# One more slot in a shared buffer pool, and a filter spectrum loaded in three parts

## The chip, the cores and the metric

The kernel runs on one core of a Trainium2 chip. The core has a matrix engine (TensorE, PE in the rows, with PEld for its weight loads), a vector engine (VectorE, DVE), an engine for casts, copies and function tables (ScalarE, ACT), a general one (GpSimd, POOL), and SyncE (SP), which issues nearly all DMA transfers in the order of its program. Each engine works through its own list of instructions in order, and waits at an instruction until the semaphores that it names have come. The metric is the device time of the program in microseconds, as the median of several executions.

## The reference

Two layers of a diffusion trunk over 640 tokens (512 latent ones and 128 of context) of width 1024. Every layer is: RMS norm and modulation, SwiGLU channel mixer, then a token mixer of three parallel parts, then a second channel mixer. The modulation (nine vectors of 1024 for each layer and each of two conditions) is a product of a condition vector with a matrix, 'adaLN' below. Cut to what matters here:

```
def fft_conv(z, k):                      # z (B, L, C), k (2L, C)
    zf = jnp.fft.rfft(z, n=2 * L, axis=1)
    kf = jnp.fft.rfft(k, n=2 * L, axis=0)
    return jnp.fft.irfft(zf * kf[None], n=2 * L, axis=1)[:, :L]

def hyena_mixer(u, sw, sb, filt, bias_d):
    v, x1, x2 = jnp.split(short_conv(u, sw, sb), 3, axis=-1)
    z = v
    for o, gate in enumerate((x1, x2)):
        z = gate * (fft_conv(z, filt[:, o]) + bias_d[o] * z)

def trunk_layer(x, cond, p, pos, ctx_kv):
    mod = silu(cond) @ p['ada_w'] + p['ada_b']
    x = x + 0.5 * g1 * swiglu(rmsnorm(x) * (1 + sc1) + sh1, ...)
    u = (rmsnorm(x) * (1 + sc2) + sh2) @ p['w_in']       # split into pool | attention | hyena
    x = x + g2 * (concat(pool, attention, hyena_mixer(...)) @ p['w_out'])
    x = x + 0.5 * g3 * swiglu(rmsnorm(x) * (1 + sc3) + sh3, ...)
```

The filter `k` depends on the weights alone. So each layer has two FFT convolutions, one after the other (`o` = 0 and 1), since the second takes the gated output of the first.

## The kernel before

**Layout.** Activations lie with features on the 128 partitions and tokens along the row. All large products are made of three matmuls each (high by high, high by low, low by high part): `split` casts a tile to its high part on ACT (L295) and takes the difference for the low part on DVE (L296). Weight tiles (`raw`, 128x512) are loaded by SP, split, and used by PE; they have pools of their own.

**The slot pool.** Almost every other temporary of the kernel comes from one pool, `sp` (L213, L227, L233): one tag, `SLOTS` = 45 buffers of 2560 bytes per partition. The buffers are handed out in rotation: a new tile takes the buffer of the tile that was allocated 45 allocations before, and its first writer waits until the last instruction that touches that older tile is done. The writer may be a DMA. SP then stands at that DMA, and every later transfer in its program with it.

**The FFT convolution** (`conv_step_old`, L1068). Both transforms are products with tables. The steps of one convolution are: SP loads four tables for the way in (`tab`, `load_full(0, 4)`, L261) and five tiles of the filter's spectrum (`kf`, `filter_tiles`, L957 to L961) that the prologue left in DRAM. PE transposes `z` (`ztp`), and ACT copies it out (`zt`, `ztc`, L1080, L1085). Two frequency halves follow (`fi` = 0 and 1): PE makes `zf` (8 products each), ACT copies the odd part (`zod`, L1100), DVE forms sum and difference (`zp`, `zm`, L1102, L1103), and `cmul` multiplies them by the filter: `zp` by `kf[fi]`, `zm` by `kf[2 + fi]`. One `cmul` is five DVE instructions (L969, L971 twice, L973, L974; tiles `cw`, `cw2`, `cy`). DVE then makes `pp` and `pmn` (L1108, L1109). The context part is multiplied by `kf[4]` (`zcs`). For the way back SP loads four more tables (`load_full(4, 8)`, L261), and PE makes `yt` from `pp`, `pmn` and these tables: the first half of the products with `pp` takes the first and the second table, the other half the third and the fourth.

**The mixer.** The two convolutions, attention and pooling are generators, and a string (`MIXP`) says in which order they are advanced. The output projection (`raw` from `in_wout`) and the first weights of the next channel mixer (`ex`) are loaded beside the second convolution.

**adaLN.** 240 dot products of 1024 elements run on DVE as one instruction each (`tensor_tensor_reduce`, L410), spread over three of the channel mixers. The instruction also writes an elementwise product that nobody reads, `junk`. Before, `junk` has one buffer of its own (128x1024 bf16, 2048 bytes per partition).

**Order.** A scheduler with priorities orders the instructions of each engine when the program is built. It knows the buffers of the pools, so a change in the number of buffers, or in what is allocated from them, moves instructions elsewhere too.

Of the kernel before, what the change touches and what calls it, by code (L numbers as in the profile page):

```python
# [13 lines left out]
BF16 = mybir.dt.bfloat16  # L14
# [3 lines left out]
P = 128  # L18
# [14 lines left out]
PROT = 8  # L33
AG0 = (1, 0, 2)
MIXT = 70
SLOTS = 45
PF = 8
WB = 5
EXB = 7
# [144 lines left out]
def hybrid_kernel(ctx: ExitStack, tc: tile.TileContext, a, depth=2, fc=22):  # L184
# [27 lines left out]
    wp = ctx.enter_context(tc.tile_pool(name="wp", bufs=4))  # L212
    sp = ctx.enter_context(tc.tile_pool(name="sp", bufs=SLOTS))  # L213
    tp = ctx.enter_context(tc.tile_pool(name="tp", bufs=2))
# [8 lines left out]
    def nm(s):  # L223
        count[0] += 1
        return f"{s}{count[0]}"

    def slot(n=NCOL, dt=F32, name="s"):  # L227
        return sp.tile([P, n], dt, tag="s", name=nm(name))
# [4 lines left out]
    def slot3(x, y, dt=F32, name="s"):  # L233
        return sp.tile([P, x, y], dt, tag="s", name=nm(name))

    def tiny(n, name="t", bufs=4):
        return tp.tile([P, n], F32, tag=f"{name}{n}", bufs=bufs, name=nm(name))
# [4 lines left out]
    def mix(n=512, name="mx"):  # L242
        return acc(n, mx, name)
# [13 lines left out]
    def load_full(q0, q1, name="tfi"):  # L257
        ts = []
        for q in range(q0, q1):
            t = slot3(2, 256, name="tab")  # L260
            DMA.dma_start(out=t.rearrange("p a b -> p (a b)"), in_=a[name][q])  # L261
            ts.append(t)
        return ts
# [24 lines left out]
    def PR(l, name):  # L288
        lo, hi = PAR_COLS[name]
        return par[l][:, lo:hi]  # L290
# [83 lines left out]
    def bias(l, g):  # L374
        return PR(l, "adab").rearrange("p (g s c r) -> p g s c r", g=9, s=2, c=4)[:, g]
# [21 lines left out]
    def ada_group(l, g):  # L397

        def load(n):
            raw = wp.tile([P, 1024], F32, tag="araw", bufs=ARAWB, name=nm("araw"))  # L400
            DMA.dma_start(out=raw, in_=a["adat"][l * 9 + g - len(AG0), n])
            ada_raw[l, g, n] = raw

        def step(n):
            raw = ada_raw[l, g, n // 2]
            i, r = n // 2, n % 2
            c, s = i // 2, i % 2
            junk = tp.tile([P, 1024], BF16, tag="junk", bufs=1, name=nm("junk"))
            with tc.issue_after(pace[0]) if pace else nullcontext():
                V.tensor_tensor_reduce(out=junk, in0=raw, in1=condb[:, r], scale=1.0, scalar=bias(l, g)[:, s, c, r:r + 1],  # L410
                                       op0=ALU.mult, op1=ALU.add, accum_out=mods[l][:, g, c, s, r:r + 1])
            if n == 2 * DC - 1:
                done.add((l, g))

        for n in range(2 * DC):
            ada_q.append(((lambda n=n: load(n // 2)) if n % 2 == 0 else None, lambda n=n: step(n)))
# [41 lines left out]
    class Norm:  # L458
# [13 lines left out]
        def stat(self, half):  # L472
            if self.key[::3] in done:
                self.affine()
            s = ssq[half]
            tot = mix(3, "tot")
            for t, o in enumerate((0, P, HT - P)):
                PE.matmul(out=tot[:, t:t + 1], lhsT=s[:, o:o + P], rhs=ones[:, 0:1], start=True, stop=True)
            var = tiny(3, "var")
            V.tensor_scalar(out=var, in0=tot, scalar1=1.0 / 1024.0, scalar2=EPS, op0=ALU.mult, op1=ALU.add)  # L480
            rs = tiny(3, "rs")
            G.tensor_tensor(out=rs, in0=var, in1=mhalf, op=ALU.pow)
            self.rs = rs
# [470 lines left out]
            self.keep(k, 4)  # L954
            yield

    def filter_tiles(l, o):  # L957
        flat = [slot3(2, 256, name="kf") for _ in range(5)]
        for j, t in enumerate(flat):
            DMA.dma_start(out=t.rearrange("p a b -> p (a b)"), in_=store[l, 2 * j + o])  # L960
        return flat  # L961

# [14 lines left out]
    def conv_step(l, o, z, gate, out):  # L977
        rl, rlc = filt[l]
        tf = [load_tables("fwd", 0, 4)]
        kf = filter_tiles(l, o)  # L980
        hb = PR(l, "hb")
        zt = [(slot3(2, 256, F32R, name="zt"), slot3(2, 256, F32R, name="ztl")) for _ in range(2)]
# [85 lines left out]
    def conv_step_old(l, o, z, gate, out):  # L1068
        rl, rlc = filt[l]
        tf = load_full(0, 4)  # L1070
        kf = filter_tiles(l, o)
        hb = PR(l, "hb")
        zt = [slot3(2, 256, name="zt") for _ in range(2)]
        for pa in range(2):
            ps = mix(512, "ztp")
            for i in range(2):
                for c in range(2):
                    t0 = pa + i * 256
                    PE.transpose(out=ps[:, (i * 2 + c) * P:(i * 2 + c + 1) * P], in_=z[c][:, t0:t0 + 255:2], identity=ident)
            S.copy(out=zt[pa].rearrange("p a b -> p (a b)"), in_=ps)  # L1080
        zc = slot(256, name="ztc")
        ps = mix(256, "ztp")
        for c in range(2):
            PE.transpose(out=ps[:, c * P:(c + 1) * P], in_=z[c][:, LAT:T], identity=ident)
        S.copy(out=zc, in_=ps)  # L1085
        yield
        pq = []
        for fi in range(2):
            fs = slice(fi * P, (fi + 1) * P)
            eo = []  # L1090
            for pa in range(2):
                ps = mix(512, "zf")
                for c in range(2):
                    for i in range(2):
                        PE.matmul(out=ps[:, c * 256:(c + 1) * 256], lhsT=tf[pa * 2 + i][:, c, fs], rhs=zt[pa][:, i, :],
                                  start=(i == 0), stop=(i == 1))
                eo.append(ps)
            with tc.high_priority(offset=min(CVP, tc.cur_priority)):
                od = slot(512, name="zod")
                S.copy(out=od, in_=eo[1])  # L1100
                zp, zm = slot(512, name="zp"), slot(512, name="zm")
                V.tensor_tensor(out=zp, in0=od, in1=eo[0], op=ALU.add)  # L1102
                V.scalar_tensor_tensor(out=zm, in0=od, scalar=-1.0, in1=eo[0], op0=ALU.mult, op1=ALU.add)  # L1103
                y = cmul(zp, kf[fi], o, 0)
                yp = cmul(zm, kf[2 + fi], o, 1)
                pp, pm_ = slot3(2, 256, name="pp"), slot3(2, 256, name="pmn")
                for q in range(2):
                    V.tensor_tensor(out=pp[:, q], in0=y[:, q], in1=yp[:, 1 - q], op=ALU.add)  # L1108
                    V.tensor_tensor(out=pm_[:, q], in0=y[:, q], in1=yp[:, 1 - q], op=ALU.subtract)  # L1109
            pq.append((pp, pm_))  # L1110
            if fi == 0:
                yield
        ti, vs = load_full(4, 8), []
        psc = mix(512, "zfc")
        for c in range(2):
            PE.matmul(out=psc[:, c * 256:(c + 1) * 256], lhsT=tcx[:, c, :], rhs=zc, start=True, stop=True)
        zcs = slot(512, name="zcs")
        S.copy(out=zcs, in_=psc)
        yc = cmul(zcs, kf[4], o, 0)
        yield  # L1120
        for c in range(2):
            cs = slice(c * P, (c + 1) * P)
            ps = mix(512, "yt")
            for pa in range(2):
                n = 0
                for fi in range(2):
                    for q in range(2):
                        PE.matmul(out=ps[:, pa * 256:(pa + 1) * 256], lhsT=pq[fi][pa][:, q, cs], rhs=ti[fi * 2 + q][:, pa, :],
                                  start=(n == 0), stop=(n == 3))
                        n += 1  # L1130
            pc = mix(128, "ytc")
            for q in range(2):
                PE.matmul(out=pc, lhsT=yc[:, q, cs], rhs=tcx[:, q, :], start=(q == 0), stop=(q == 1))
            v = slot(T, name="yv")
            S.activation(out=v[:, 0:LAT].rearrange("p (t a) -> p a t", a=2), in_=ps.rearrange("p (a t) -> p a t", a=2),
                         func=AF.Identity, scale=rl[:, o * 2 + c:o * 2 + c + 1])
            S.activation(out=v[:, LAT:T], in_=pc, func=AF.Identity, scale=rlc[:, o * 2 + c:o * 2 + c + 1])
            vs.append(v)
        yield
        gate = gate()  # L1140
        for c in range(2):
            u, v = slot(T, name="yu"), vs[c]
            V.scalar_tensor_tensor(out=u, in0=z[c], scalar=hb[:, o * 2 + c:o * 2 + c + 1], in1=v, op0=ALU.mult, op1=ALU.add)
            w = slot(T, name="yw")
            V.tensor_tensor(out=w, in0=u, in1=gate[c], op=ALU.mult)
            out.append(w)
        yield
# [663 lines left out]
```

## Time and profile before

| what | value |
|---|---|
| median of 3 runs | 2406.22 us (2406.14 to 2408.6) |
| profiled execution, its own time | 2408.28 us |
| its span, first to last instruction | 2406.5 us |
| PE busy | 2363.9 us, 98% |
| DVE busy | 1919.6 us, 80% |
| ACT busy | 1094.1 us, 45% |
| mean traffic | 112 GB/s |
| mean granted clock of TensorE | 0.993 |

The span is what the rows' times count in; the execution's own time is 1.78 us longer than it. PE is busy for nearly all of the span, so the places where it stands still are the ones to look at; each idle piece is listed with the instruction or transfer that ended it.

### The profile page before, as it was taken

What the parts mean: (1) busy time and instruction counts of PE and PEld (TensorE: products, weight loads), DVE (VectorE), ACT (ScalarE), POOL (GpSimd) and SP (SyncE); (2) the same over time, 40 slices, a digit from 0 to 9 for tenths busy, and PEclk for the clock granted to TensorE, in tenths of its full rate; (3) what the DMA queues carried; (4) which work ended last, traced back from release to release, by engine and by line L of the source; (5) the groups of instructions that cost most, each with busy time, mean ns of one, the idle gap of its engine ahead of it and who ended that gap; (6) DMA issues with size and microseconds to landing.
All of it is one profiled execution on the core that took longest, in us unless ns stands there. A gap on an engine that the chain in (4) does not pass through costs nothing.

```text
span 2406.5 us, 41068 instructions
## 1 busy us (share of the span) xinstructions
PE 2363.9 (98%) x15576; PEld 2240.9 (93%) x15576; DVE 1919.6 (80%) x3885; ACT 1094.1 (45%) x2228; POOL 18.2 (1%) x46
## 2 busy tenths in 40 slices
PE   8999999999989999999999999999998999999999
PEld 3799999999877999999999999999987799999999
DVE  7888888996786798888989889898778678567583
ACT  4654352534345553453535435253434555335251
POOL 0000000000000000000000000000000000000000
PEclk9999999999989999999999999999999999999999
DMA  9434434353310235344343343534231022222222
GB/s 320 173 101 128 134 117 155 107 172 114 102 45 14 71 110 162 124 125 144 115 137 108 119 136 115 166 110 158 91 112 54 18 71 80 79 84 78 85 68 90
DMA packets 132646, 270.37 MB, mean 112 GB/s; under 512 B 15002, under 2 KB 24924, under 8 KB 132320
## 3 DMA queue, kind: packets, MB, share of 16 engines
q1 hardware_dynamic: 132448, 267.75, 34.8%
q8 instruction: 122, 2.00, 0.4%
q14 instruction: 76, 0.62, 0.1%
HBM read 259.56 MB, written 8.13 MB: 111 GB/s over the span
## 4 chain that ended last, share of the span: by engine, by line
PE 88%; DVE 6%; issue 2%; DMA 1%; ACT 1%; SPq 1%; POOL 0%; POOLq 0%; DVEq 0%; ACTq 0%
PE mm L205 74%; PE Z L205 5%; PE yt L205 1%; PE o L205 1%; PE pt L209 1%; DVE junk L410 1%; PE fk L205 1%; PE mx L205 1%; PE ada L205 1%; PE zf L205 1%; DVE kwl L296 0%; DMA kf<-store 0%; DVE wlo L296 0%; PE rsb L205 0%; DVE rp L1308 0%
## 5 line engine op out<-in xcount | busy, mean ns | idle before, releaser
L205 PE MATMUL mm<-hhi,whi 128*128 128x320 f32 x1440 | 448.4, 311 | 1.1 <-ACT u L1224 1.1
L295 ACT CAST whi<-raw 128x512 fp32r<-128x512 f32 (+1 forms) x394 | 238.7, 606 | 463.3 <-PE mm L205 423.0
L205 PE MATMUL mm<-hlo,whi 128*128 128x320 f32 x1440 | 446.3, 310 | 0.0
L205 PE MATMUL mm<-hhi,wlo 128*128 128x320 f32 x1440 | 446.0, 310 | 0.0
L205 PE MATMUL mm<-alo,whi 128*128 128x320 f32 x1198 | 370.8, 310 | 0.8 <-DVE alo L296 0.8
L205 PE MATMUL mm<-ahi,whi 128*128 128x320 f32 x1198 | 370.8, 310 | 0.0
L205 PE MATMUL mm<-ahi,wlo 128*128 128x320 f32 x1198 | 370.7, 309 | 0.0
L296 DVE TENSOR_TENSOR wlo<-raw,whi 128x512 fp32r<-128x512 f32 (+1 forms) x394 | 263.3, 671 | 75.7 <-ACT whi L295 71.3
L410 DVE CUSTOM_DVE_ANT_0 junk<-araw,condb,par 128x1024 bf16<-128x1024 f32 x240 | 307.4, 1281 | 2.1 <-DMA araw<-in_adat 0.8
L205 PEld LDWEIGHTS mm<-hhi,whi 128*128 128x128 f32 x1440 | 270.5, 188 | 5.9 <-ACT u L1224 2.8
L205 PEld LDWEIGHTS mm<-hlo,whi 128*128 128x128 f32 x1440 | 270.8, 188 | 1.9 <-issue 1.8
L205 PEld LDWEIGHTS mm<-hhi,wlo 128*128 128x128 f32 x1440 | 270.5, 188 | 1.4 <-issue 1.4
L205 PE MATMUL mm<-tlo,whi 128*128 128x320 f32 x864 | 267.4, 309 | 0.0
L205 PE MATMUL mm<-thi,whi 128*128 128x320 f32 x864 | 267.4, 309 | 0.0
L205 PE MATMUL mm<-thi,wlo 128*128 128x320 f32 x864 | 267.3, 309 | 0.0
L205 PEld LDWEIGHTS mm<-alo,whi 128*128 128x128 f32 x1198 | 225.0, 188 | 1.0 <-DVE alo L296 1.0
L205 PEld LDWEIGHTS mm<-ahi,whi 128*128 128x128 f32 x1198 | 225.0, 188 | 0.1
L205 PEld LDWEIGHTS mm<-ahi,wlo 128*128 128x128 f32 x1198 | 225.0, 188 | 0.0
L295 ACT CAST whi<-ex 128x512 fp32r<-128x512 f32 x216 | 134.2, 621 | 188.0 <-PE mm L205 175.6
L296 DVE TENSOR_TENSOR wlo<-ex,whi 128x512 fp32r<-128x512 f32 x216 | 149.2, 691 | 32.6 <-ACT whi L295 28.4
L295 ACT CAST whi<-ws 128x512 fp32r<-128x512 f32 x144 | 89.4, 621 | 162.2 <-PE mm L205 123.1
L205 PEld LDWEIGHTS mm<-thi,whi 128*128 128x128 f32 x864 | 162.3, 188 | 0.0
(263 smaller groups left out, 4704.2 us busy)
## 6 DMA issues: line engine op xcount, KB each, us to landing
araw<-in_adat SPq DMA_DIRECT2D x120, 512.0 KB, 3.6
raw<-in_wgu SPq DMA_DIRECT2D x208, 256.0 KB, 3.1
ex<-in_wgu SPq DMA_DIRECT2D x144, 256.0 KB, 2.7
raw<-in_wd SPq DMA_DIRECT2D x128, 256.0 KB, 2.7
raw<-in_win SPq DMA_DIRECT2D x56, 256.0 KB, 3.0
ar<-in_ada SPq DMA_DIRECT2D x48, 256.0 KB, 5.4
raw<-in_wd SPq DMA_DIRECT2D x64, 192.0 KB, 2.6
tab<-in_tfi SPq DMA_DIRECT2D x32, 256.0 KB, 3.9
```

The costliest lines, as they stand in the source:

```text
L205: cls.order(nc.tensor.matmul(**k))
L209: cls.order(nc.tensor.transpose(**k))
L295: S.copy(out=hi, in_=src)
L296: V.tensor_tensor(out=lo, in0=src, in1=hi.bitcast(F32), op=ALU.subtract)
L410: V.tensor_tensor_reduce(out=junk, in0=raw, in1=condb[:, r], scale=1.0, scalar=bias(l, g)[:, s, c, r:r + 1], op0=ALU.mult, op1=ALU.add, ac ...
```

## The change

Three things: `SLOTS` goes from 45 to 46; `junk` is allocated from the slot pool (and the buffers of one tiny tile, `var`, go from four to two); and the five loads of the filter's spectrum are made in three parts, tiles 0 and 2 at the start of the convolution, 1 and 3 after the matmuls of the first frequency half, tile 4 after those of the second.

```
-SLOTS = 45
+SLOTS = 46
...
-            junk = tp.tile([P, 1024], BF16, tag="junk", bufs=1, name=nm("junk"))
+            junk = slot(1024, BF16, "junk")
...
-            var = tiny(3, "var")
+            var = tiny(3, "var", 2)
...
-    def filter_tiles(l, o):
-        flat = [slot3(2, 256, name="kf") for _ in range(5)]
-        for j, t in enumerate(flat):
+    def filter_tiles(l, o, which=range(5)):
+        flat = {j: slot3(2, 256, name="kf") for j in which}
+        for j, t in flat.items():
             DMA.dma_start(out=t.rearrange("p a b -> p (a b)"), in_=store[l, 2 * j + o])
...
-        kf = filter_tiles(l, o)
+        kf = filter_tiles(l, o, (0, 2))
...
+            if fi == 0:
+                kf.update(filter_tiles(l, o, (1, 3)))
+            else:
+                kf.update(filter_tiles(l, o, (4,)))
```

The allocations of a convolution thus come in another order, and with 46 buffers in the rotation each tile of a mixer takes the buffer of another predecessor. (Line numbers after the change are 4 higher from L1099 on.)

The first place is SP's program around the second convolution of layer 0, from the loads of its spectrum to the tables of the way back. Before:

```order
L960 DMA kf_7156<-store 128x512 [waits DMAHW6_49]
L960 DMA kf_7157<-store 128x512 [waits DMAHW7_49,PE_49]
L960 DMA kf_7158<-store 128x512 [waits DMAHW0_49,Activation_49]
L960 DMA kf_7159<-store 128x512 [waits DMAHW1_49,PE_49]
L960 DMA kf_7160<-store 128x512 [waits DMAHW2_49,PE_49]
L301 DMA raw_7911<-in_wout 128x512 [waits DMAHW3_49,DVE_49]
...
L261 DMA tab_7531<-in_tfi 128x512 [waits DVE_49]
L261 DMA tab_7533<-in_tfi 128x512 [waits DMAHW5_49]
L261 DMA tab_7535<-in_tfi 128x512 [waits DMAHW6_49,DVE_49,Activation_49]
L261 DMA tab_7537<-in_tfi 128x512 [waits DMAHW7_49,DVE_49]
```

And after the change:

```order
L960 DMA kf_7156<-store 128x512 [waits DMAHW6_49]
L960 DMA kf_7157<-store 128x512 [waits DMAHW7_49,PE_49]
L301 DMA raw_7911<-in_wout 128x512 [waits DMAHW0_49,DVE_49]
...
L587 DMA ex_9861<-in_wgu 128x512 [waits DMAHW4_49,DVE_49]
L960 DMA kf_7272<-store 128x512 [waits DMAHW5_49,PE_49]
L960 DMA kf_7273<-store 128x512 [waits DMAHW6_49,Activation_49]
...
L960 DMA kf_7501<-store 128x512 [waits DMAHW2_49,PE_49]
L301 DMA raw_8341<-in_wout 128x512 [waits DMAHW3_49,DVE_49]
L261 DMA tab_7531<-in_tfi 128x512 [waits DMAHW4_49,DVE_49]
L261 DMA tab_7533<-in_tfi 128x512 [waits DMAHW5_49,DVE_49]
```

Three of the five spectrum loads stand behind three `in_wout` and two `ex` loads. The first table of the way back, `tab_7531`, waits on DVE in both programs, but for another instruction: the semaphore's count is that of L971 (`cw2` of `zm` in the second half) before, and of L974 in the `cmul` before it (`cy` of `zp`) after; `tab_7533` has no such wait before, and after waits for the L971 that held the first table.

The second place is ACT's program at the start of that convolution, where it copies the transposed `z` out. Before:

```order
L1303 COPY qkc_6800<-u_6832 128x128
L295 CAST whi_7727<-raw_7725 128x512
L1080 COPY zt_7166<-ztp_7168 128x512
L1080 COPY zt_7167<-ztp_7174 128x512
L1085 COPY ztc_7180<-ztp_7181 128x256
```

And after:

```order
L1307 COPY qkc_6800<-u_6832 128x128
L1080 COPY zt_7160<-ztp_7162 128x512
L1080 COPY zt_7161<-ztp_7168 128x512
L1085 COPY ztc_7174<-ztp_7175 128x256
L295 CAST whi_7727<-raw_7725 128x512
```

The weight cast `whi` has moved behind the three copies, and on DVE its difference `wlo_7728` has moved behind the first three of four rotary instructions. In PE's program the matmuls that use this weight come after the `zf` products in both. In the three channel mixers that carry adaLN work, the order on DVE, SP and PE also differs in many places: the low parts of activations (`alo`, L296) now stand ahead of dot products (L410) that stood ahead of them, and groups of products are exchanged as a whole.

## Rows read from the trace of the kernel before

**Rows 1.** PE idle pieces added up by what ended them (total, times, longest us).
```profile
PE yt L205 <- DVE wlo L296: 8.3, 2, 4.2
PE pt L209 <- DVE sc L1357: 7.6, 4, 3.6
...
PE zf L205 <- ACT zt L1080: 2.1, 2, 1.0
...
PE tot L205 <- DVE sq L455: 1.0, 1, 1.0
```

**Rows 2.** Busy time by stretch: PE, PEld, DVE, ACT, POOL, clock, DMA share, GB/s.
```profile
300.00:500.00 200.00, 200.00 (x1366) 200.00 (x1365) 176.56 (x313) 91.48 (x171) 1.07 (x3) 1.00 0.41 128
500.00:545.00 45.00, 43.93 (x300) 43.35 (x299) 42.19 (x90) 14.91 (x30) 0.85 (x1) 1.00 0.53 171
...
640.00:680.00 40.00, 34.28 (x197) 29.71 (x196) 33.82 (x75) 13.51 (x30) 0.28 (x4) 1.00 0.41 140
```

**Rows 3.** Timeline of layer 0 at the way back: start, duration, engine, line.
```profile
673.91 0.68 DVE L969 TENSOR_TENSOR cw<-zp,kf 128x512 f32<-128x512 f32 x1
...
675.52 0.42 DVE L974 TENSOR_TENSOR cy<-cw 128x256 f32<-128x256 f32 x1
...
676.46 0.76 DVE L971 TENSOR_TENSOR cw<-zm,kf 128x256 f32<-128x256 f32 x2
677.24 1.75 SPq L261 DMA_DIRECT2D tab<-in_tfi  x4
...
680.07 1.81 PE L205 MATMUL yt<-tab,pp 128*128 128x256 f32 x4 [4.17 <-DVE wlo L296]
680.15 0.69 DVE L969 TENSOR_TENSOR cw<-zcs,kf 128x512 f32<-128x512 f32 x1
...
682.37 1.62 PE L205 MATMUL yt<-tab,pp 128*128 128x256 f32 x3 [0.50 <-DMA tab<-in_tfi]
```

**Rows 4.** The same place in layer 1, from SP, PE and DVE.
```profile
1827.85 1.75 SPq L261 DMA_DIRECT2D tab<-in_tfi  x4
...
1830.60 3.51 PE L205 MATMUL yt<-tab,pp 128*128 128x256 f32 x8 [4.10 <-DVE wlo L296]
...
1827.07 0.76 DVE L971 TENSOR_TENSOR cw<-zm,kf 128x256 f32<-128x256 f32 x2
```

**Rows 5.** Timeline of layer 0 at the start of the second convolution.
```profile
646.02 2.33 SPq L960 DMA_DIRECT2D kf<-store  x5
648.47 4.30 SPq L301 DMA_DIRECT2D raw<-in_wout  x3
657.58 0.93 SPq L587 DMA_DIRECT2D ex<-in_wgu  x2
...
651.06 0.62 ACT L295 CAST whi<-raw 128x512 fp32r<-128x512 f32 x1
651.59 1.07 ACT L1080 COPY zt<-ztp 128x512 f32<-128x512 f32 x2
651.71 0.69 DVE L296 TENSOR_TENSOR wlo<-raw,whi 128x512 fp32r<-128x512 f32 x1 [1.03 <-DMA kf<-store]
652.22 1.56 PE L205 MATMUL zf<-zt,tab 128*128 128x256 f32 x6 [1.04 <-ACT zt L1080]
```

**Rows 6.** Clock after the two stalls, by stretches of 2 us (columns as in rows 2).
```profile
680.00:682.00 2.00, 1.81 (x4) 0.80 (x4) 2.00 (x6) 0.45 (x1) 0.14 (x2) 0.67 0.99 338
...
684.00:686.00 2.00, 2.00 (x6) 1.56 (x6) 1.68 (x5) 0.82 (x2) 0.14 (x2) 0.50 0.00 0
686.00:688.00 2.00, 2.00 (x9) 1.69 (x8) 1.79 (x7) 0.30 (x1) 0.00 (x0) 0.62 0.02 4
...
1834.00:1836.00 2.00, 2.00 (x11) 1.73 (x10) 1.83 (x5) 0.82 (x2) 0.14 (x2) 0.90 0.00 0
```

**Rows 7.** The dot products of adaLN, and the transfers of their operand (KB, us to landing).
```profile
L410 DVE CUSTOM_DVE_ANT_0 junk<-araw,condb,par 128x1024 bf16<-128x1024 f32 x240 | 307.4, 1281 | 2.1 <-DMA araw<-in_adat 0.8
...
araw<-in_adat SPq DMA_DIRECT2D x120, 512.0 KB, 3.6
```

## The prediction

> **What bounds the kernel now.** I began with the busy shares: PE 98% of the span, DVE 80%, ACT 45%, so only what PE does, or where it stands still, sets the time. The second view was the list of PE's waits, added up by what ended them [rows 1]. It is short, and its two largest entries are in the mixers, twice each because there are two layers: 8.3 us before the products `yt` (way back of an FFT convolution) and 7.6 us before `pt` (softmax). The third view was the busy time by stretch [rows 2]. In the channel mixers PE has no idle time (200.00 of 200.00 us) while DVE is busy for 176.56, so DVE has 12% to spare there and a microsecond more or less on it costs nothing as long as PE has its next operands. In the mixer around the second convolution PE works 34.28 of 40 us. A change that moves loads and buffers can gain only in such places, and can lose in all of them.
>
> The last view was the timeline of the place with the longest wait [rows 3]. The wait of 4.17 us is put down to DVE `wlo`, but that is only the semaphore that came last by the profile. Read down the rows: DVE ends its third product (L971) at 676.46 + 0.76 = 677.22, SP issues the first table of the way back at 677.24, PE starts `yt` at 680.07. So SP had been standing at that load, which waits for the buffer that L971 reads, and 680.07 - 677.24 = 2.83 us is the way of a table from issue to use. A second wait of 0.50 us at 682.37 is for the later tables. In layer 1 the same three marks are 1827.83, 1827.85 and 1830.60 [rows 4], 2.75 us. So this stall is one of buffers: the table comes late because its slot comes free late.
>
> The Trainium skill (Perfetto Trace Analysis, Optimization Strategy) says that the same gap coming back on the engine that should be full can mean that there is no room for the next tile. The trace agrees for `yt` (4.2 us, twice, behind a slot), and not for `pt`, which comes back too and waits for DVE's `sc`.
>
> **The change part by part.**
>
> *The tables of the way back.* With the new rotation the first table waits for L974 of the first `cmul` instead, which ends at 675.52 + 0.42 = 675.94 [rows 3]: 677.24 - 675.94 = 1.30 us earlier. The second table takes over the wait for L971 (677.22, before: third in line behind nothing), so it gains little: it was issued at 677.24 + 1.75 / 4 = 677.68, now at 677.22, that is 0.46 us earlier. The third has no wait for DVE any more, and the fourth one for L973, behind L971 by about 0.35 us, so both follow the second in line: third 677.66 against 678.11, fourth 678.10 against 678.55. The first half of the `yt` products needs the first two tables in turn, the second half the other two. What the end of `yt` gains is thus between 0.45 us (the last table's issue) and 1.30 us (the first's); and since the first load now starts 1.3 us ahead of the others instead of four within 1.75 us, the last ones meet less traffic (338 GB/s in this stretch [rows 6]), which should give some tenths. Between 0.45 and 1.30 I take 0.9.
>
> *The start of the second convolution.* Before, ACT casts a weight (`whi`, 651.06, 0.62 us) and then copies `zt` (651.59); PE waits 1.04 us for the copy [rows 5]. After, the copies come first. They wait for PE's transposes alone, which are done when ACT is free at 651.06 at the latest, so `zf` starts 651.59 - 651.06 = 0.53 us earlier. On DVE, `wlo` (651.71, 0.69 us, after 1.03 us of waiting) stood ahead of the four rotary instructions and now stands behind three of them, so these start up to 1.03 us earlier, less what `wlo` then costs between the third and the fourth: its 0.62 us, and some 0.3 us for ACT's cast that now comes behind 1.07 + 0.39 us of copies. I put DVE's gain at 0.6 us and, as PE's chain and DVE's chain must both come earlier, the place at 0.55 us. It can't be more than 1.04, and it is nothing if the matmuls with this weight came to wait; they stand behind the `zf` products, over 4 us later.
>
> *The spectrum.* Five loads within 2.33 us become two, with three `in_wout` loads ahead of the rest [rows 5]. Tiles 1 and 3 are then issued behind `ex`, which before went out at 657.58, and are first read at 673.91 [rows 3]: 15 us, against a landing time of a few. Tile 4 is issued near the `in_wout` loads before the tables and first read at 680.15. I cost the delay at nothing, since the cover is over 10 us; if it went, the first load late costs its own landing, 2.8 us as for the tables, a time. The loads that move forward, three `in_wout`, are early already.
>
> So per layer 0.9 + 0.55 = 1.45 us for these two, in all 2.9 us. Does it reach the end? After `yt` PE is busy until the softmax wait, and that one follows from PE's own products through ACT and DVE, so it moves with PE and stays as long. The first layer's gain is carried through channel mixers in which PE has no gaps, so nothing takes it back.
>
> *junk in a slot, and 46 slots.* Each of the 240 dot products (1281 ns) [rows 7] now takes one of the shared slots for its 1.3 us. Before it waited for its predecessor alone, on the same engine, so never. The new wait is for a tile allocated 46 allocations before, mostly read by an earlier DVE instruction: nothing. But as 240 more tiles go through the same rotation, every other tile in these channel mixers finds its predecessor 46 allocations back to be younger than with 45 and no junk. With 12% of DVE idle and PE without gaps, I cost it at 0, with bounds of -1.0 (the 0.97 us wait before `tot` at the end of the first channel mixer goes, [rows 1], where DVE is busy 42.19 of 45 us [rows 2]) and +3.6 (one operand of a dot product comes late there and DVE stands behind its load [rows 7]). The prologue and the first convolution keep their order on PE, and I cost them at 0.
>
> The sum against the profiled execution: span 2406.5 - 2.9 = 2403.6; with the 1.78 us around it 2405.4. That execution (2408.28) is 2.06 us above the median of the runs shown, so for the median: 2406.22 - 2.9 = 2403.3.
>
> **The rivals.**
>
> *The low clock goes too.* After the 4.17 us wait TensorE's granted clock fell in the trace to 0.50, the lower of its two levels (1.2 of 2.4 GHz), from about 680.7 (0.67 over 680 to 682) to 686 at least [rows 6], and in layer 1 until shortly after 1834 (0.90 over 1834 to 1836). The same eight `yt` records that take 3.51 us behind the wait in layer 1 [rows 4] show what is at stake: at the full clock they would take half. If the shorter wait kept the clock up, layer 0 would save half of the low stretch of at least 5.3 us, 2.65 us, and layer 1 half of those 3.51, 1.75 us: 2403.3 - 4.4 = 2398.9. Against it: even then PE stands for about 2.9 us and again for the later tables, so most of 675 to 681 remains idle. The Trainium skill (TensorE: Matmul & The Clock Gate, HAM oscillation) says that each gap which is long enough starts the next products cold again, and only shorter ones leave the clock; by that rule a shorter gap can be worth more than its length, and the trace bears out the first half (0.50 behind the long waits) but has no wait of this length in the mixers.
>
> *Nothing arrives.* The first table comes 1.3 us earlier, but the products wait for the third and fourth instead, and what the earlier start gives is lost there; at the start of the convolution PE's 1.04 us turn into a longer wait for DVE at the next products. Then the gain is the 0.45 us of the last table per layer at most: 2405.3 to 2406.2, say 2405.8. For it speaks that before PE already waited 0.50 us for a later table.
>
> *Slower.* The dot products sit at the head of DVE's list with a wait for a slot or for an operand that SP issues later than before, and behind them stand the differences `alo` and `wlo` that PE needs within a few products. It decides from the point where DVE's lag passes PE's lead; the end of a channel mixer is the likeliest place (DVE 42.19 of 45 us). Three stretches carry such work; with one stall of a 3.6 us landing in each, 10.8 - 2.9 = +7.9 us, 2414.1; with two, +4.3, 2410.5. For it: 240 new slot users against one new slot. Against it: DVE has 23 us to spare in every 200.
>
> *The change does not do what it says.* If the 46th slot only feeds junk, nothing is left for the mixers. But no dot product runs in the mixers, and the way the table's wait moved is there in the order of slots. I count it with the second rival.
>
> **How the numbers follow.** Forecast, 1.2 to 4.8 us faster: 0.48. Low clock gone too, wholly or in part: 0.20. Nothing arrives, within 1.2 us: 0.17. Slower: 0.15, of it 0.13 by more than 4.8 us and the rest by less. What a measurement of this kernel can tell from no change is about 0.2%, 4.8 us. The forecast and the second rival lie inside it, save a small part of the forecast's upper end (0.05) that goes to faster: faster 0.25, same 0.62, slower 0.13. The range from 2398.5 holds the low clock's case almost wholly, and up to 2409.0 the milder half of the slower one; what is left out is about 0.05 below and 0.1 above. By the bounds of the terms alone (per layer 0.45 to 1.30 for the tables, 0 to 1.04 for the start, once -1.0 to +3.6 for junk) the forecast itself runs from 2400.5 to 2408.9.
>
> **What would show it.** SP's first table of the way back issued at the start of the second `cmul` instead of its third product, and PE's wait before `yt` near 3 instead of 4.2 us; the wait before `zf` near 0.5 us; `pt` still 3.6 us; no new entry of over 1 us in PE's list of waits from the channel mixers. Were PE to wait for `kf` products (`pp`, `cy`) or `alo` in several places, the forecast would be wrong to the slow side; were the clock at 1.00 behind `yt`, to the fast side.

## The result, and the profile after

The changed kernel takes 2424.86 us (median of 4 runs, 2424.5 to 2425.51) against 2406.48 us of the kernel before beside it: a ratio of 1.0070, 95% interval 1.0054 to 1.0086. It is 18.4 us slower by these medians, 16.8 us (13.0 to 20.7) by the ratio, outside the predicted range and on the side to which the prediction gave 0.13.

The span grew from 2406.5 to 2423.4 us, 16.9 us. PE's waits in the changed kernel, added up by what ended them (total, times, longest), answer to [rows 1]:

```profile
PE mm L205 <- DVE kwl L296: 8.5, 3, 2.8
PE pt L209 <- DVE sc L1361: 7.6, 4, 3.6
...
PE yt L205 <- DMA tab<-in_tfi: 3.3, 3, 3.0
PE yt L205 <- DVE pp L1112: 2.9, 1, 2.9
...
PE tot L205 <- DVE sq L455: 1.4, 1, 1.4
...
PE zf L205 <- ACT zt L1080: 0.8, 2, 0.4
```

What the prediction wanted in the mixers is there: `yt` waits 2.9 to 3.0 us each time in place of 4.2, `zf` 0.4 in place of 1.0, `pt` as long as before. But the longest entry is new: three waits of 2.8 us for `kwl`, the low parts of down-projection weights, at the ends of the three channel mixers that carry adaLN work. `yt` <- DVE `pp` is layer 1's table wait under another name; the releasers' names are a guess by the last semaphore.

This list adds up to 43.0 us of idle PE after and 38.0 before, so 5 of the 16.9 us. The rest is seen when both programs' matmuls are numbered (15,576 in each) and the start of the same number is compared. Their order differs within groups of products, so a step of a few tenths may be off, not a microsecond. The body of a channel mixer is its long first stretch (108 to 500 us for the first one), the end is what follows up to the next stage:

```
stretch                              later than before at its end   what it adds
prologue                                    0.14                      +0.1
first channel mixer, layer 0, body          1.98                      +1.8
its end                                     7.24                      +5.3
mixer of layer 0                            4.18                      -3.1
second channel mixer, layer 0, body         6.68                      +2.5
its end                                    10.96                      +4.3
first channel mixer, layer 1, body         13.00                      +2.1
its end                                    17.46                      +4.5
mixer of layer 1                           16.87                      -0.6
second channel mixer, layer 1              16.85                       0.0
```

So there are three parts: the mixers give 3.7 us, the ends of three channel mixers take 14.0, and their bodies 6.4 in many small steps. The last channel mixer, which has no adaLN work, is unchanged to a few hundredths.

**The ends.** SP, ACT, DVE and PE at the end of the first channel mixer, after:

```profile
502.72 7.29 SPq L401 DMA_DIRECT2D araw<-in_adat  x3
511.49 0.80 SPq L320 DMA_DIRECT2D raw<-in_wd  x2
...
513.39 1.02 ACT L295 CAST kwh<-raw 128x512 fp32r<-128x512 f32 x2
...
514.95 1.28 DVE L410 CUSTOM_DVE_ANT_0 junk<-araw,condb,par 128x1024 bf16<-128x1024 f32 x1
516.15 0.08 DVE L410 DVE_READ_ACCUMULATOR2_ANT mod<- 128x1 f32 x1
516.15 1.28 DVE L410 CUSTOM_DVE_ANT_0 junk<-araw,condb,par 128x1024 bf16<-128x1024 f32 x1
517.35 0.09 DVE L410 DVE_READ_ACCUMULATOR2_ANT mod<- 128x1 f32 x1
517.35 1.16 DVE L296 TENSOR_TENSOR kwl<-raw,kwh 128x512 fp32r<-128x512 f32 x2
...
518.10 0.41 PE L205 MATMUL mm<-ahi,kwl 128*128 128x320 f32 x1 [2.84 <-DVE kwl L296]
```

And the same place before, SP first, then DVE:

```profile
500.86 2.98 SPq L401 DMA_DIRECT2D araw<-in_adat  x2
506.82 0.80 SPq L320 DMA_DIRECT2D raw<-in_wd  x2
...
511.43 1.28 DVE L410 CUSTOM_DVE_ANT_0 junk<-araw,condb,par 128x1024 bf16<-128x1024 f32 x1
512.63 0.08 DVE L410 DVE_READ_ACCUMULATOR2_ANT mod<- 128x1 f32 x1
512.63 1.16 DVE L296 TENSOR_TENSOR kwl<-raw,kwh 128x512 fp32r<-128x512 f32 x2
```

On DVE two dot products of 1.28 us stand directly ahead of that `kwl` pair (one before), with no idle time between. Counted over DVE's whole list, 74 dot products stand ahead of it, and 72 in the kernel before; at the other two ends it is 158 against 156 and 234 against 232. ACT has cast the weights of this pair by 514.41, and PE stands from 515.26 to 518.10, so it waits for DVE's turn alone. DVE is not waiting there at all; it does the wrong thing first.

SP also differs: it has three operand loads of dot products in a row where it had two, and each must wait for a dot product to free its buffer, so the pair of weight loads behind them goes out at 511.49 instead of 506.82. But in the order of loads and casts that pair belongs to the next `kwl` pair, which runs from 518.89, and not to the one that PE waits for.

A stall of 2.84 us can cost more than itself. The clock after the second one, by stretches of 2 us (busy PE, PEld, DVE, ACT, POOL, then granted clock):

```profile
1235.00:1237.00 2.00, 0.47 (x3) 0.47 (x4) 2.00 (x5) 0.00 (x0) 0.00 (x0) 1.00 0.50 182
1237.00:1239.00 2.00, 2.00 (x11) 2.00 (x10) 1.47 (x3) 0.00 (x0) 0.00 (x0) 0.59 0.91 284
1239.00:1241.00 2.00, 2.00 (x10) 2.00 (x10) 0.00 (x0) 0.89 (x2) 0.00 (x0) 0.56 1.03 381
1241.00:1243.00 2.00, 2.00 (x15) 2.00 (x14) 1.84 (x4) 1.23 (x3) 0.00 (x0) 1.00 0.14 46
```

At 0.59 and 0.56 PE does 11 and 10 matmuls in 2 us instead of 15, a loss of 2 x 2 - 2 x (0.59 + 0.56) = 1.7 us. The wait itself is 2.84 us where it was 0.10 before. Together that is 4.4 us; the table has 4.3. Behind the first one the clock stayed at 1.00; there it fell 23 us later, behind the wait for `tot` (0.51 over 541 to 543 us).

**The bodies.** Before and after, 108 to 500 us of the first channel mixer:

```profile
108.00:500.00 392.00, 392.00 (x2675) 392.00 (x2674) 338.47 (x619) 181.07 (x346) 1.07 (x3) 1.00 0.40 127
```

```profile
108.00:500.00 392.00, 392.00 (x2663) 390.19 (x2662) 334.56 (x616) 179.00 (x346) 1.26 (x3) 1.00 0.39 125
```

PE is busy for 392.00 of 392 us in both, yet it does 2663 matmuls in place of 2675. Twelve matmuls at 0.147 us (392 / 2675) are 1.8 us, the step of the table. The loss is in single matmuls that come 0.21 to 0.28 us behind their predecessor instead of 0.147, so the row's modelled ends cover it; only the weight loads' column (390.19) shows a gap. The Trainium skill (Trainium Kernel Development and Optimization, Performance Expectations) says that matmul busy time is a bad measure and names the weight loads' busy share as one of the good ones; here the trace agrees.

The weight loads also name what PE waited for in this stretch: `rc`, the copy that ACT (L616) makes of an accumulator and DVE (L621) adds to. First before, then after (busy, mean ns, idle time ahead and what ended it); 0.5 and 1.3 us are the whole 1.8:

```profile
L205 PEld LDWEIGHTS mm<-hhi,whi 128*128 128x128 f32 x280 | 52.6, 188 | 0.0
...
L205 PEld LDWEIGHTS mm<-thi,whi 128*128 128x128 f32 x216 | 40.6, 188 | 0.0
```

```profile
L205 PEld LDWEIGHTS mm<-hhi,whi 128*128 128x128 f32 x280 | 52.5, 188 | 0.5 <-DVE rc L621 0.5
...
L205 PEld LDWEIGHTS mm<-thi,whi 128*128 128x128 f32 x216 | 40.5, 188 | 1.3 <-ACT rc L616 0.7
```

DVE's groups in the same stretch show where DVE lost time, first before, then after (same columns):

```profile
L296 DVE TENSOR_TENSOR alo<-pr,ahi 128x640 fp32r<-128x640 f32 x22 | 18.1, 822 | 0.0
```

```profile
L410 DVE CUSTOM_DVE_ANT_0 junk<-araw,condb,par 128x1024 bf16<-128x1024 f32 x64 | 80.9, 1281 | 0.0
...
L296 DVE TENSOR_TENSOR alo<-pr,ahi 128x640 fp32r<-128x640 f32 x22 | 18.2, 825 | 13.1 <-ACT ahi L295 12.9
```

The dot products themselves wait for nothing here (0.0). But `alo` now makes DVE stand 13.1 us for ACT's cast `ahi`, 0.6 us each. In DVE's list of before, 57 of the 104 `alo` have a dot product directly ahead of them, which covers ACT's cast; after, 3 have, and 56 have it directly behind. How the 13.1 us of DVE turn into 1.8 us of late `rc` is not traced step by step.

### The profile page after: what moved, and what is told of

Same layout as the page of the kernel before. It is cut to its first block, busy times and chain, and to the rows that moved or that the text cites. A ratio compares the mean times of both kernels' runs of the same rounds, so it can differ in the third digit from the quotient of the medians.

```text
span 2423.4 us, 41012 instructions
## 1 busy us (share of the span) xinstructions
PE 2375.9 (98%) x15576; PEld 2246.0 (93%) x15576; DVE 1912.7 (79%) x3885; ACT 1090.1 (45%) x2228; POOL 18.6 (1%) x46
## 5 line engine op out<-in xcount | busy, mean ns | idle before, releaser
L296 DVE TENSOR_TENSOR wlo<-raw,whi 128x512 fp32r<-128x512 f32 (+1 forms) x394 | 263.4, 672 | 78.0 <-ACT whi L295 76.1
L410 DVE CUSTOM_DVE_ANT_0 junk<-araw,condb,par 128x1024 bf16<-128x1024 f32 x240 | 302.7, 1280 | 1.3 <-DMA araw<-in_adat 1.3
L296 DVE TENSOR_TENSOR wlo<-ex,whi 128x512 fp32r<-128x512 f32 x216 | 149.1, 690 | 29.8 <-ACT whi L295 25.2
L205 PEld LDWEIGHTS mm<-tlo,whi 128*128 128x128 f32 x864 | 162.2, 188 | 0.0
```

The source lines that it names most:

```text
L205: cls.order(nc.tensor.matmul(**k))
L296: V.tensor_tensor(out=lo, in0=src, in1=hi.bitcast(F32), op=ALU.subtract)
```

## The experiments

Nine kernels, each timed in five rounds beside the kernel before. The ratio tells the sum. For the parts, the profiled execution of each is compared with that of before by the numbers of its matmuls, as above (us that each stretch adds):

```
                 prologue  body 1  end 1  mixer 0  body 2  end 2  body 3  end 3  mixer 1
changed kernel      0.1     1.8     5.3    -3.1     2.5     4.3     2.1     4.5    -0.6
junk45             -0.2     1.8     5.7    -2.3     2.8     5.5     1.8     4.5     1.1
split45             5.1     0.0     2.2    -2.0     0.3     0.0    -1.1     0.0     0.2
junk46             -3.8     1.8     4.3    -2.5     2.4     4.3     2.2     4.8     1.5
group46             5.7     0.2    -0.1    -3.2     0.0     0.0    -0.8     0.0    -0.5
own_alofirst       -1.0     1.8     0.9    -1.5     2.7     0.1     2.0     0.1     3.2
pair46             -0.3     1.0     3.8    -3.6     1.6     2.3     0.9     4.1    -0.3
group46five        -1.2     0.2     0.0    -2.2     0.0     0.0     0.0     0.3     1.1
body46             -1.1     1.8     0.3    -1.9     2.6     0.0     2.2     0.1     0.7
tail46              3.8     0.2     4.9    -2.1     0.0     4.3    -0.7     5.7     0.1
```

The prologue and the two mixer columns must be read with care: junk45 and own_alofirst leave the tables' and `zf`'s waits as they were, and still stand at -2.3 and 1.1, -1.5 and 3.2. What differs there is how long the clock stays low behind the same stalls: over 660 to 730 us the mean granted clock is 0.90 before, 0.95 in junk45 and 0.93 in own_alofirst, over 1815 to 1890 us it is 0.95, 0.93 and 0.89. So a single execution tells a mixer to 2 or 3 us only; PE's waits there are steadier.

**junk alone, 45 slots.**

```
-            junk = tp.tile([P, 1024], BF16, tag="junk", bufs=1, name=nm("junk"))
+            junk = slot(1024, BF16, "junk")
```

> Only junk moves to the shared slots (45 of them, five spectrum loads at once). Theory 1, the loss comes from the order that the scheduler gives DVE once each dot product takes a slot of its own: all of it is here, 6.4 us of small steps in the three channel mixers and 14.0 us at their ends, and nothing of the gain in the mixers, so 2406.5 + 20.4 = 2427 us, with kwl waits of 2.8 us three times. Theory 2, the loss comes from the later spectrum loads or from the other rotation of 46 slots: about 2406 us, no kwl waits.

Measured: 2430.28 us, ratio 1.0087 (1.0071 to 1.0103). Its three waits for `kwl` are those of the changed kernel:

```profile
PE mm L205 <- DVE kwl L296: 8.5, 3, 2.8
```

The whole loss is in this one line of the change; 46 slots and the split loads are not needed for it.

**The split loads alone** (45 slots, `junk` in its own buffer).

> Only the spectrum is loaded in three parts (45 slots, junk in its own buffer). Theory 1: the channel mixers stay as before, the wait before zf falls from 1.04 to 0.4 us in both layers and the table wait stays at 4.2 us: 2405.3 us (2404.5 to 2406.2). Theory 2 (later loads hurt): waits for spectrum or projection weights, 2410 us or more.

Measured: 2407.41 us, ratio 0.9988 (0.9976 to 1.0000), 2.9 us faster than the kernel before where 0.9 was expected. No `kwl` stall, and the bodies stay within 0.3 us of before but for one that is 1.1 faster; the 2.2 us at the first end are a wait of 1.6 us for `tot` (1.0 before) and a low clock behind it. `yt` waits 4.4 and 4.3 us, much as before, `zf` 0.4. Theory 2 is out: the later loads cost nothing that shows.

**46 slots and junk in them, five loads at once.**

> 46 slots and junk in them, five spectrum loads at once. Theory 1: the loss of the channel mixers as in the changed kernel (20.4 us) and the earlier tables, but zf's wait at 1.0 us: 2406.5 + 20.4 - 2.5 = 2424.4 us, about as the changed kernel. Theory 2, where the split causes the loss: 2404 us.

Measured: 2426.14 us, ratio 1.0068 (1.0052 to 1.0085), the time of the whole change: what the split adds is below what these times can tell.

**The whole change, with one slot for each group of 16 dot products.**

```
-            junk = slot(1024, BF16, "junk")
+            if n == 0 or (l, g) not in junks:
+                junks[l, g] = slot(1024, BF16, "junk")
+            junk = junks[l, g]
```

> The whole change, but junk takes one slot for each group of 16 dot products, which write it one after the other, in place of one slot each: as before, every dot product then follows its predecessor on the same tile. Theory 1 (order): DVE's order is again that of before, the kwl waits and the small steps go, the gain of the mixers stays: 2406.5 - 3.7 = 2402.8 us. Rival, the occupied slot itself is the price (the group holds one for longer than a single dot product would): still 10 us or more slower than before.

Measured: 2406.16 us, ratio 0.9984 (0.9973 to 0.9996), 3.9 us faster than the kernel before and the only version here whose interval lies wholly below 1. `var` has its two buffers here too, and they cost nothing that shows. In DVE's list 55 `alo` have a dot product ahead again, and its wait is back to

```profile
L296 DVE TENSOR_TENSOR alo<-pr,ahi 128x640 fp32r<-128x640 f32 x21 | 17.2, 821 | 0.8 <-ACT ahi L295 0.8
```

A slot is occupied for longer than in the changed kernel, so the occupied slot is not the price. The bodies cost 0.2 us at most, the ends nothing.

**The order alone: junk in its own buffer, 45 slots, dot products issued only behind the `alo` that precedes them in the program.**

```
             act = slot(T, F32R, "ahi"), slot(T, F32R, "alo")
-            split(self.pr, *act)
+            hi, lo = act
+            S.copy(out=hi, in_=self.pr)
+            i = V.tensor_tensor(out=lo, in0=self.pr, in1=hi.bitcast(F32), op=ALU.subtract)
+            pace[:] = [i.ins]
             return act
```

> The kernel before (45 slots, junk in its own buffer, five loads at once), but each dot product may be issued only behind the difference alo that precedes it in the program: DVE's order has alo directly ahead of a dot product in 53 places (8 before, 56 in the changed kernel). No slot is touched. If order alone makes the small steps: about 6 us of them in the three channel mixers, alo idle on ACT's ahi of about 13 us by the first one; and if the lag of DVE makes the kwl waits at the ends too, 20 us in all (2426). If the ends come from where the slots put the dot products there, only the 6 us: 2412. If order is harmless and the slots' waits are the price: 2406.

Measured: 2414.74 us, ratio 1.0030 (1.0016 to 1.0043). DVE's wait in the first body:

```profile
L671 DVE TENSOR_TENSOR alo<-pr,ahi 128x640 fp32r<-128x640 f32 x18 | 14.9, 825 | 13.0 <-ACT ahi L670 12.9
```

13.0 us, with no slot touched, and the bodies cost 1.8, 2.7 and 2.0 us, as in the changed kernel; in the first body the late matmuls are the same 18. So the bodies' loss is order alone. The ends cost 0.9, 0.1 and 0.1 us, without `kwl` stalls (0.4 us in two waits): the ends have another cause than the lag of the bodies.

**Two dot products share a slot** (120 slots instead of 240).

> The whole change, but two dot products that read the same operand tile share one slot: 120 slots in place of 240. The order has a dot product directly ahead of alo in 34 places (57 before, 3 in the changed kernel). If the loss follows this order, the small steps are about half, 3 us, and the whole lies between group46 and the changed kernel, 2410 to 2418; if it is the first dot product of a pair that counts wherever it stands, as the changed kernel, 2424.

Measured: 2418.22 us, ratio 1.0041 (1.0027 to 1.0056). 34 `alo` have a dot product ahead, the bodies cost 1.0, 1.6 and 0.9 us, about half, and the waits at the ends shrink to

```profile
PE mm L205 <- DVE kwl L296: 6.1, 3, 2.0
```

The loss goes with the number of slots that the dot products take.

**46 slots with shared junk, five loads at once.**

> group46 with the five spectrum loads at once: what the 46th slot does alone. The tables of the way back are issued 1.3 us earlier, zf's wait stays at 1.04 us: against the kernel before -2.5 us (-1 to -3.5), that is 1 us slower than group46. If the gain of the mixers is the split's alone: no difference from before, 0 us.

Measured: 2407.49 us, ratio 0.9992 (0.9979 to 1.0004), within what can be told from no change. The waits divide cleanly (the tables' about 3 us as in group46, `zf`'s 1.0 as before), but the times don't: group46's 3.9 us can't be shared out between slot and split, as the intervals overlap.

**Dot products with slots of their own in the body only, and at the end only** (the last of five groups).

```
-            if n == 0 or (l, g) not in junks:
+            if not last or n == 0:        # body; the other kernel has: if last or n == 0
```

> The whole change with the dot products' slots split by place: of the five groups in each of the three channel mixers the first four take a slot for every dot product, the last group (the end of the mixer) one slot for all. DVE's order has alo ahead of the dot products as in the changed kernel, and the end as before. Theory: 6.5 us of small steps, no kwl waits, the mixers' gain of 3.7 kept: 2 to 4 us slower than the kernel before. If the lag of the small steps is what causes the kwl waits, these come here too, and it is 15 us slower.

> The reverse: the first four groups share a slot each, in the last group every dot product takes its own. The order of the body is that of before, at the end two and three dot products stand ahead of kwl and SP has three operand loads in a row ahead of the weights. Theory: kwl waits of 2.8 us three times, each with a stretch at the low clock, 14 us, less the mixers' 3.7: 8 to 11 us slower than before. If the ends need the lag of the body to be late: no kwl waits, and as group46, 3.9 us faster.

Measured: body 2411.57 us, ratio 1.0007 (0.9995 to 1.0019), 1.7 us slower than before where 2 to 4 were expected; end 2418.79 us, ratio 1.0041 (1.0026 to 1.0055), 9.9 us slower where 8 to 11 were expected. The waits for `kwl` in the first and in the second:

```profile
PE mm L205 <- DVE kwl L296: 0.4, 2, 0.2
```

```profile
PE mm L205 <- DVE kwl L296: 8.5, 3, 2.8
```

Against group46, which has neither, the body costs (1.0007 - 0.9984) x 2406 = 5.5 us and the end (1.0041 - 0.9984) x 2406 = 13.7 us. Their sum with group46's -3.9 us is +15.3 us, against +16.8 (1.0070) for the whole change; each of these differences is good to some 4 us. Within that, the two losses are separate and add up.

At the ends the wait goes with the number of dot products ahead of `kwl` in DVE's list: 2.8 us with two more than before (changed kernel, junk45, junk46, tail46), 2.0 us with one more (pair46), 0.2 at most with as many as before (the other five). No run changed that order with the slots untouched; that the order is the price there, and not a wait for a slot, rests on this and on DVE's rows, which have no idle time ahead of those dot products.

## Why the prediction was wrong, point by point

*The tables of the way back: right.* Predicted for layer 0: first table 1.30 us earlier against DVE's third product, the last 0.45. After, SP issues behind L974, and PE follows:

```profile
682.50 2.57 SPq L261 DMA_DIRECT2D tab<-in_tfi  x4
...
682.04 0.42 DVE L974 TENSOR_TENSOR cy<-cw 128x256 f32<-128x256 f32 x1
...
682.98 0.76 DVE L971 TENSOR_TENSOR cw<-zm,kf 128x256 f32<-128x256 f32 x2
...
685.27 1.19 PE L205 MATMUL yt<-tab,pp 128*128 128x256 f32 x2 [2.97 <-DMA tab<-in_tfi]
```

L971 ends at 683.74: the first issue is 1.24 us ahead of it (0.02 behind it before, [rows 3]), and the last ends 1.33 us behind it (1.77 before), 0.44 earlier. From first issue to use it is 2.77 us (2.83 before). PE's wait fell by 1.2 us and the next one from 0.50 to 0.18, more than the 0.9 taken: the last table lands 3.1 us after its issue, where it took 4.3 before, 1.2 us less, where the prediction gave it "some tenths".

*The start of the second convolution: right.* PE's wait for `zf` fell from 1.04 to 0.38 us, and the next one, for `u`, from 0.57 to 0.39 ([rows 5] for the first): 0.84 us against 0.55. The waits for `yt`, `zf` and `u` together fell by 4.2 us over both layers, where 2.9 was forecast. In time the 2.9 stands beside 3.7 in this pair of executions, and beside group46's 3.9 (1.0 to 6.5) by the ratio, where nothing else changed to speak of. That the times come so close is partly luck: a mixer of one execution is good to 2 or 3 us only, and group46's interval is wide.

*The low clock.* It did not stay up behind the shorter wait in either layer (0.50 over 686 to 690 us in layer 0). In layer 1 TensorE ran longer at the lower level (1.2 of 2.4 GHz) than before:

```profile
1846.00:1848.00 2.00, 1.76 (x3) 1.00 (x4) 2.00 (x7) 0.56 (x2) 0.14 (x2) 0.50 0.94 338
1848.00:1850.00 2.00, 2.00 (x6) 1.41 (x5) 2.00 (x6) 0.24 (x1) 0.00 (x0) 0.50 0.58 161
1850.00:1852.00 2.00, 2.00 (x6) 1.60 (x6) 1.90 (x4) 0.28 (x1) 0.14 (x2) 0.56 0.00 0
```

Some 4 us behind the stall's end it was at 0.90 before [rows 4, 6], here at 0.56, which took back most of what layer 1's shorter waits gave (1.9 us of waits, 0.6 in the table). As junk45 and own_alofirst show, such a stretch differs between kernels with the same stall, so it is not laid to the change.

*The spectrum: right.* The only entry of the waits that names `kf` lies in the prologue and is 1.6 us before and after, and the split alone was not slower.

*junk in a slot: the step that failed.* The prediction put it at 0, with +3.6 us as the upper bound: "With 12% of DVE idle and PE without gaps, I cost it at 0". It costs 19 to 21 us (junk45: 0.0087 x 2406 = 20.9; body and end apart: 5.5 + 13.7 = 19.2). Three things were wrong in it. First, it asked what the dot products would wait for, and found rightly that this is next to nothing (0.0 us ahead of them in the first body). It did not ask what their new place in DVE's list does to their neighbours, although the change of order was in view: `alo` ahead of the dot products makes DVE wait for ACT (13.1 us in one body), and two more dot products ahead of `kwl` make PE wait for DVE (2.84 us, three times). Second, 12% of idle DVE time is an average; at the end of a channel mixer DVE is busy for 42.19 of 45 us [rows 2], which the prediction read but used in its bounds for one stall in one mixer, though the other two ends are as full (40.38 of 45 us from 1214, 43.29 from 1651, before). Third, a stall was priced at its length, while about 1.7 us at the low clock came on top at each of these ends, for which [rows 6] had the price.

*The slower rival* named the place (the ends of the three channel mixers), the victim (the differences behind the dot products) and, for three stalls, +7.9 us. Its mechanism, a dot product that waits for a slot or an operand at the head of DVE's list, is not what happened, and the small steps were not in it. It was half the size, and had too small a chance.

*What stays open.* Why the scheduler places the dot products elsewhere once each has a slot (behind `alo` in the bodies, two more of them ahead of `kwl` at the ends) is argued, not shown. Counted in the order of allocation, 138 of the 240 find a tile of another kind (`pr`, `ahi`, `thi` and others) 46 allocations before, many of which have readers on other engines too; with their own buffer it is always another dot product. Sharing a slot among 2 or 16 gives half and nearly none of the effect, which fits.

## What to carry to other kernels

When a throwaway output moves into a shared rotating pool, its allocations can become dependencies on unrelated tiles (here 138 of 240), and the order of the engines may change with it even where the trace then shows no wait for those tiles; give such outputs one tile for many instructions. Where the order of an engine changes, price the neighbours of what moved: what did it cover before, and what stands behind it now. And a full busy column of PE does not say that nothing was lost: compare the count of matmuls in the same stretch, and price a stall with the clock that follows it.

## What the runs showed of the hardware

The clock in the prologue differs between executions of programs in which PE's matmuls have the same order there (up to 294 us in all kernels here). 24 to 32 us of group46's profiled run, and of the kernel before:

```profile
24.00:32.00 8.00, 8.00 (x30) 2.39 (x29) 4.29 (x9) 3.95 (x7) 0.00 (x0) 0.50 1.05 384
```

```profile
24.00:32.00 8.00, 8.00 (x33) 2.65 (x32) 5.25 (x12) 4.09 (x8) 0.00 (x0) 1.00 1.05 383
```

By the prologue's end group46 is 5.7 us behind, more than its whole gain. That is why its profiled span (2407.7 us) is longer than that of the kernel before (2406.5), though its time over 12 runs is shorter.

A stop of PE of 2.84 us in a stretch where it was otherwise full was followed by a granted clock of 0.59 and 0.56 at the second end, and of 1.00 at the first. At the way back of the convolution the clock went to 0.50 behind 4.2 us as well as behind 2.9 us.
